# Softmax attention in four stages: dividing the products with the values, one pair of heads at a time, in place of the probabilities

## The chip, the cores and the metric

The kernel runs on one core of a Trainium2 chip. The metric is device time in microseconds (us) for one execution of the whole program.

The engines have short names below: PE is the matrix engine (TensorE), PEld its weight loads, DVE VectorE, ACT ScalarE, POOL GpSimd and SP the engine that issues the loads.

## What is computed

Two small transformer networks run one after the other over 256 context tokens and 256 latent tokens of width 1024. The first has feed-forward layers round two mixers: an even one (global attention beside an RWKV-7 recurrence) and an odd one (window attention with a sink). The second has two mixers: latent attention beside an mLSTM, and gated linear attention (GLA) beside neighbourhood attention. All is in float32, and a product of float32 matrices in the large projections is made of three products of high and low parts.

Each of the four attentions is a softmax over the keys and a product with the values:

```python
def attend(q, k, v):
    s = jnp.einsum('bqhgd,bkhd->bhgqk', q, k).astype(jnp.float32)
    p = jax.nn.softmax(s, axis=-1).astype(v.dtype)
    return jnp.einsum('bhgqk,bkhd->bqhgd', p, v)
```

Three of them scale the products by 1/8, the latent attention by 1/sqrt(96). The window attention has one more logit for each head, the sink, which counts in the sum but has no value.

## The kernel before

One helper, `attend`, makes all four attentions. It is a generator. Its unit of work is one head of a pair and one block of 128 queries, against n keys (256, 384 or 512), so that a pair of heads has four units. For a unit, `scores` makes the products of queries and keys on PE (`ps_s`, L725), takes the maximum of every row on DVE (L730), multiplies it by -scale on DVE (L732, or L734 with a sink), has ACT form the exponentials with their sum (L735), and lets DVE take the reciprocal of the sum (L739) and multiply the unit's 128 x n exponentials by it (L740). Two units later, `turn` transposes these on PE in pieces of 128 x 128 (`ps_ptr`, L751), and ACT copies the result from PSUM (L754). When the four units of a pair are turned, `values` multiplies them with the values on PE (`ps_o`, L760; 128 rows for the pair, 256 queries) and calls the stage's `out`, which takes the result from PSUM: a copy on DVE in the first two stages (L790, L1178), a product with the gate `z` on DVE in the last two (L1452, L1664).

The work is written as generators that take turns (`weave`), and a list scheduler then sets the order of the instructions on each engine. What keeps an order are the data, and the rings of tiles: a pool's tag with `bufs` buffers hands out the next buffer only when its last reader has ended. The tag `nt` of the pool `normp` has four buffers of 128 x 256. In the kernel before it serves the norms (L448), a rotary embedding (`qsw`, L1116), the mLSTM's `u` and `sq` (L1512), and the gates of the last mixer (`zt`, L1627).

The four stages, by the times of the profile:

- Stage 1, 557 to 667 us: 32 units, 16 of 512 keys and then 16 of 256, in turns with `features` of RWKV-7 (L834 to L874, mostly DVE).
- Stage 2, 1779 to 1866 us: 32 units of 384 keys with a sink, in turns with the projection of the queries and half of the output projection (`ps_pr`).
- Stage 3, 2268 to 2382 us: 32 units, 16 of 256 keys and then 16 of 512, in turns with four heads of the mLSTM (`ps_gl` L1474, `ps_sm` L1493, `ps_h` L1506, `ps_ht` L1529) and then the output projection.
- Stage 4, 2594 to 2652 us: 16 units of 512 keys, in turns with the GLA and then the output projection.

These are 112 units and 28 pairs of heads in all.

Of the kernel before, what the change touches and what calls it, by code (L numbers as in the profile page):

```python
# [17 lines left out]
KD = 8  # L18
# [8 lines left out]
def weave(*gens):  # L27
    """run generators in turns; each a generator or (generator, steps per turn)"""
    gens = [g if isinstance(g, tuple) else (g, 1) for g in gens]
    while gens:  # L30
        for g in list(gens):
            for _ in range(g[1]):
                try:
                    next(g[0])
                except StopIteration:
                    gens.remove(g)
                    break


def weave_first(gen, *gens):  # L40
    """all in turns until the first has ended"""
# [6 lines left out]
def every(gen, n):  # L48
    """n steps of gen for one"""
# [5 lines left out]
def until(gen, mark):  # L55
    """the steps of gen as far as the mark; gen can go on from there"""
# [6 lines left out]
class Banks:  # L63
    """pools as one: their tiles in turns"""
# [10 lines left out]
class Net:  # L75
    def __init__(self, es, tc, ins, out):
# [7 lines left out]
        self.hp = p("h", 1)  # the normed stream while a phase multiplies it, other things of its size after  # L84
# [6 lines left out]
    def setup(self):  # L91
# [18 lines left out]
        self.unit = self.const.tile([128, 2, 32], F32, name="unit")  # ones in the first column, in the second  # L110
# [21 lines left out]
    def ring(self, es, raw, split):  # L132
        """for the length of a phase, more of the tiles [128, 1024] that weights go through"""
# [4 lines left out]
    def wtile(self, tag, dt):  # L138
        """in turns from the rings that there are, by their lengths"""
# [11 lines left out]
    def wload(self, w, r0, kt, c0, n):  # L151
        """rows r0.. (kt tiles of 128), columns c0..c0+n of w as (high, low) [128, kt, n]"""
# [12 lines left out]
    def order(self, later, earlier):  # L165
        """the instruction goes after the other one, of the same engine"""
        self.tc.add_manual_dep(later.ins, earlier.ins.name, mybir.DependencyInfo(mybir.DependencyClass.NoSync, mybir.DependencyReason.DATA), reason="order")

    def mm3(self, ps, a, b, first, last):
        """ps += a.T @ b; a, b: (high, low) pairs"""  # L170
# [13 lines left out]
    def proj_steps(self, h, w, c0, ncols, n, done, r0=0, kt=KD, tok=slice(0, 512)):  # L184
        """done(m, psum [128, n]) for each 128 columns of h.T @ w[:, c0:c0+ncols], features on partitions"""
# [14 lines left out]
    def fetch(self, items):  # L200
        """for heads(): items (w, c0, m, done) of 128 columns each"""
        return [(self.wload(w, 0, KD, c0, 128), self.psa.tile([128, 512], F32, tag="a", name="ps_pr"), m, done) for w, c0, m, done in items]

    def heads(self, h, tiles, segs, end=True):
        """done(m, psum [128, 512]) for fetch()'s tiles, the tokens of one segment before those of the next;
        not at the end if other segments follow"""
# [13 lines left out]
    def behind(self, gen, n=99):  # L220
        """n steps of products, on TensorE after what is there so far"""
# [4 lines left out]
    def proj_t_steps(self, h, w, c0, ncols, toks, done, kt=KD):  # L226
        """done(tile, psum [128, ncols]) for each 128 tokens, tokens on partitions"""
# [18 lines left out]
    def opening(self, mod, items, segs):  # L246
        """heads() for the first layer: its modulation vectors in four parts of two tiles of features each, the products of
        a part as it comes"""
# [6 lines left out]
        for f in range(4):  # L255
            ps = self.psm.tile([128, 512], F32, tag="m", name="ps_mod")
            for r in range(2):
                for a in range(2):  # rows of the result: shift or scale, tile, conditioning
# [30 lines left out]
    def mod_steps(self, name, w, fixes, gain=None, start=0):  # L289
        """silu(c) @ w + b for both conditionings to M[name], in steps; fixes: {chunk: (mul, add)}"""  # L290
# [3 lines left out]
        for g in range(start, (nch_all + 3) // 4):  # L294
# [3 lines left out]
            # products and sums over tiles of rows on VectorE; rows: (conditioning, column of a pair), pair  # L298
            for h in range(nch // 2):
                acc = [self.accp.tile([128, 1024], F32, tag=f"acc{i}", name="acc", bufs=1) for i in range(2)]  # L300
                for k in range(KD):
                    v = tile(k, 2 * h)
                    for i in range(2):
                        if k:
                            nc.vector.scalar_tensor_tensor(acc[i], v, cs[:, k, i:i + 1], acc[i], ALU.mult, ALU.add)  # L305
                        else:
                            a = nc.vector.tensor_scalar(acc[i], v, cs[:, k, i:i + 1], None, ALU.mult)
                            if start and (g, h) == (start, 0):  # after opening()
# [32 lines left out]
    def psum(self, es, a, n=1, m=1, x=0, side="left"):  # L341
        """the PSUM pools of a phase: banks for products, norms, modulation, other things"""
# [7 lines left out]
    def tick(self, n=1, left=99):  # L350
        """n steps of the modulation vectors; no group of columns is begun with less than 8 of them left"""
# [13 lines left out]
    def rstd(self, src, ngroups, ones, ntok, eps, dst, psp=None, scale=1.0):  # L365
        """dst [128 tokens, ntok/128, ngroups] = 1 / sqrt(scale * ones' sums of src [128, ntok] (or of several) over partitions + eps)"""
# [11 lines left out]
    def bcast(self, ps, src):  # L378
        """ps [128, 128 tokens] = src [128 tokens, 1] on every partition"""
# [1767 lines left out]
```

## Time and profile before

| | |
|---|---|
| three timed runs | 2671.02, 2678.37, 2682.64 us; median 2678.37 |
| span of the profiled execution, by which all times below are read | 2679.4 us, 1.0 above the median; no other time of it is on record |
| busy over the span: PE, DVE, ACT, POOL | 95%, 66%, 38%, 25% |
| chain of work that ended last: PE, DVE, ACT | 83%, 10%, 3% |

The span is that of one execution under the profiler. The busy share of an engine is a mean over stages that differ, so each of the four stages is read by itself. The granted clock of PE (PEclk) is 1.00 at 2.4 GHz; at its lower level, 1.2 GHz, it is 0.50, and a figure between them is a mean over a stretch in which it had both.

### The profile page before, as it was taken

Reading aid. Unit: us, or ns where it says so; the run is one execution under the profiler, and the core shown is the slowest. Engines: PE = TensorE matmul, PEld = TensorE weight load, DVE = VectorE, ACT = ScalarE, POOL = GpSimd, SP = SyncE. Lnnn points to the kernel's source line nnn. Section 1 sums busy time; section 2 is a strip of 40 time slices with the busy share of each in tenths; the row PEclk is TensorE's granted clock in tenths of the full one; section 3 lists DMA queues with packets and bytes.
Section 4 is the critical chain, followed back from the end, with each engine's and each line's share of the span. In section 5 each row is a group of like instructions: output and inputs, shape, how many; then the busy total and the mean of one; then the engine's idle time right before and its main releaser. Section 6 shows DMA issues by size and latency. Waiting matters only on the chain.

```text
span 2679.4 us, 47406 instructions
## 1 busy us (share of the span) xinstructions
PE 2539.3 (95%) x19372; PEld 2079.3 (78%) x19372; DVE 1764.7 (66%) x2852; ACT 1016.9 (38%) x1916; POOL 672.7 (25%) x665
## 2 busy tenths in 40 slices
PE   7999999998878999999999999999999999999898
PEld 5777789854666887777897777885999887569675
DVE  4967745467666676778586877377554652765885
ACT  3322225345223252222242122366534643645454
POOL 2420322033333143113243113230414120012331
PEclk9999999988787989999999999999999999899999
DMA  8756643100000265566555666241665231023312
GB/s 263 222 175 210 183 123 98 32 0 1 3 4 27 81 180 182 180 194 198 151 149 166 211 186 185 79 132 43 182 186 150 76 103 47 16 67 105 88 48 71
DMA packets 426505, 321.32 MB, mean 120 GB/s; under 512 B 16784, under 2 KB 400528, under 8 KB 426288
## 3 DMA queue, kind: packets, MB, share of 16 engines
q1 hardware_dynamic: 426288, 318.30, 40.5%
q8 instruction: 152, 2.49, 0.4%
q14 instruction: 65, 0.53, 0.1%
HBM read 317.21 MB, written 1.05 MB: 119 GB/s over the span
## 4 chain that ended last, share of the span: by engine, by line
PE 83%; DVE 10%; ACT 3%; issue 2%; DMA 1%; POOL 1%; DVEq 0%; ACTq 0%; SPq 0%; POOLq 0%
PE ps_ff L172 9%; PE ps_ff L173 9%; PE ps_ff L174 9%; PE ps_pr L172 7%; PE ps_pr L173 6%; PE ps_pr L174 6%; PE ps_fo L172 5%; PE ps_fo L173 5%; PE ps_fo L174 5%; PE ps_s L725 3%; PE ps_o L760 2%; PE ps_w L976 2%; PE ps_ptr L751 1%; PE ps_st L1028 1%; DVE wl L157 1%
## 5 line engine op out<-in xcount | busy, mean ns | idle before, releaser
L156 ACT CAST wh<-wr 128x1024 fp32r<-128x1024 f32 (+2 forms) x402 | 417.0, 1043 | 990.5 <-PE ps_ff L173 415.6
L157 DVE TENSOR_TENSOR wl<-wr,wh 128x1024 fp32r<-128x1024 f32 (+2 forms) x402 | 521.4, 1301 | 396.1 <-ACT wh L156 393.0
L172 PE MATMUL ps_ff<-h,wh 128*128 128x512 f32 (+1 forms) x1232 | 451.9, 367 | 0.5 <-ACT fu L536 0.5
L173 PE MATMUL ps_ff<-h,wh 128*128 128x512 f32 (+1 forms) x1232 | 451.1, 366 | 0.0
L174 PE MATMUL ps_ff<-h,wl 128*128 128x512 f32 (+1 forms) x1232 | 450.5, 366 | 0.6 <-DVE wl L157 0.6
L420 POOL TENSOR_SCALAR uh<-fu 128x512 fp32r<-128x512 f32 (+1 forms) x88 | 169.3, 1924 | 774.0 <-DVE fu L537 774.0
L174 PE MATMUL ps_pr<-h,wl 128*128 128x256 f32 (+2 forms) x920 | 305.8, 334 | 12.9 <-DVE wl L157 12.8
L172 PE MATMUL ps_pr<-h,wh 128*128 128x256 f32 (+2 forms) x920 | 305.7, 337 | 7.2 <-ACT wh L156 4.5
L173 PE MATMUL ps_pr<-h,wh 128*128 128x256 f32 (+2 forms) x920 | 305.6, 334 | 2.5 <-POOL h L457 1.5
L305 DVE SCALAR_TENSOR_TENSOR acc<-wr,csa,acc 128x1024 f32<-128x1024 f32 x224 | 296.8, 1365 | 3.9 <-DMA wr<-in_w_mod_dram 3.9
L172 PE MATMUL ps_fo<-uh,wh 128*128 128x512 f32 (+1 forms) x824 | 278.9, 340 | 0.0
L173 PE MATMUL ps_fo<-uh,wh 128*128 128x512 f32 (+1 forms) x824 | 278.7, 339 | 0.0
L174 PE MATMUL ps_fo<-uh,wl 128*128 128x512 f32 (+1 forms) x824 | 277.7, 338 | 0.0
L172 PEld LDWEIGHTS ps_ff<-h,wh 128*128 128x128 f32 x1232 | 231.6, 188 | 51.6 <-ACT wh L156 6.7
L174 PEld LDWEIGHTS ps_ff<-h,wl 128*128 128x128 f32 x1232 | 231.6, 188 | 42.2 <-DVE wl L157 1.0
L173 PEld LDWEIGHTS ps_ff<-h,wh 128*128 128x128 f32 x1232 | 231.7, 188 | 40.5
L174 PEld LDWEIGHTS ps_pr<-h,wl 128*128 128x128 f32 x920 | 177.4, 193 | 30.6 <-DVE wl L157 14.5
L172 PEld LDWEIGHTS ps_pr<-h,wh 128*128 128x128 f32 x920 | 176.9, 194 | 28.0 <-ACT wh L156 8.2
L173 PEld LDWEIGHTS ps_pr<-h,wh 128*128 128x128 f32 x920 | 177.5, 194 | 20.3 <-POOL h L457 2.2
L172 PEld LDWEIGHTS ps_fo<-uh,wh 128*128 128x128 f32 x824 | 155.0, 188 | 26.7 <-issue 8.4
L173 PEld LDWEIGHTS ps_fo<-uh,wh 128*128 128x128 f32 x824 | 155.0, 188 | 18.8 <-issue 0.8
L174 PEld LDWEIGHTS ps_fo<-uh,wl 128*128 128x128 f32 x824 | 154.9, 188 | 18.2
(615 smaller groups left out, 4335.4 us busy)
## 6 DMA issues: line engine op xcount, KB each, us to landing
wr<-in_ffn_in_dram SPq DMA_DIRECT2D x176, 512.0 KB, 4.6
wr<-in_w_mod_dram SPq DMA_DIRECT2D x144, 512.0 KB, 4.4
wr<-in_ffn_out_dram SPq DMA_DIRECT2D x88, 512.0 KB, 4.3
wr<-in_l_w_in_dram SPq DMA_DIRECT2D x55, 512.0 KB, 3.8
wr<-in_l_w_mod_dram SPq DMA_DIRECT2D x48, 512.0 KB, 4.3
wr<-in_even_w_in_dram SPq DMA_DIRECT2D x21, 512.0 KB, 4.1
wr<-in_l_w_out_dram SPq DMA_DIRECT2D x16, 512.0 KB, 4.1
wr<-in_even_w_out_dram SPq DMA_DIRECT2D x14, 512.0 KB, 4.1
```

The costliest lines, as they stand in the source:

```text
L156: a = nc.scalar.copy(hi[:, : kt * n], raw)
L157: b = nc.vector.tensor_tensor(lo[:, : kt * n], raw, hi[:, : kt * n].bitcast(F32), ALU.subtract)
L172: mm(ps, a[0], b[0], start=first, stop=False)
L173: mm(ps, a[0], b[1], start=False, stop=False)
L174: self.mm = mm(ps, a[1], b[0], start=False, stop=last)
L305: nc.vector.scalar_tensor_tensor(acc[i], v, cs[:, k, i:i + 1], acc[i], ALU.mult, ALU.add)
L420: nc.gpsimd.tensor_scalar(hi, src, 1.0, None, ALU.mult)
L725: nc.tensor.matmul(s, q(h, q0s[b]), k(h), start=True, stop=True)
L751: nc.tensor.transpose(tr[:, j * 128:(j + 1) * 128], e[:, j * 128:(j + 1) * 128], self.ident)
L760: nc.tensor.matmul(o[64 * par:64 * par + 64, :nq], v(2 * m + par, j), PT[m, par][:, j, :nq], start=j == 0, stop=j == nk - 1, tile_position ...
L976: nc.tensor.matmul(out(rw, b), lhsT[rw, cl], rhs(rw, cl), start=True, stop=True, tile_position=(32 * q, 32 * q))
L1028: nc.tensor.matmul(Sv[half[par], d, m], TM[h, ks[d], d, m], S[h, par, d, m], start=True, stop=True, tile_position=(64 * (1 - par), 64 * par))
```

## The change

The exponentials stay as they are. The sums of a pair's four units are kept together in a tile `den`, and `values` takes the reciprocals of all four columns at once (DVE, L767 of the changed kernel), spreads each over 64 columns in a tile `rw` (ACT, L769), transposes that on PE into the unused half of the bank of `ps_o` (L771), copies it back to SBUF as `rbs` (ACT, L774), and hands it to `out`. In stages 1 and 2 `out` now multiplies where it copied. In stages 3 and 4 POOL first multiplies the gate by `rbs`, and DVE's product stays. `rw` and `rbs` are tiles of the `nt` ring. In stage 1 the scale 1/8 goes into the gain of the queries, and the maximum is taken with its sign turned, so that the product with -scale falls away there.

Over the program this takes 112 reciprocals and 112 multiplications of exponentials from DVE, and 32 products with -scale. It adds on DVE 28 reciprocals of 128x4, on ACT 56 copies of 128x256, on PE 56 transposes and on POOL 12 products of 128x256. The order of ACT has 34 loads of an activation table where it had 32. Docstrings and comments are gone too, which changes no instruction.

```diff
+            qg8 = T("qg8", [128, 1])
+            nc.vector.tensor_scalar(qg8, qg, 0.125, None, ALU.mult)
...
-                done_q = done_qk(qt, qg)
+                done_q = done_qk(qt, qg8)
...
+        den = {}
...
-            nc.vector.tensor_reduce(mx[:, 0:1], s, AX.X, ALU.max)
-            if sink is None:
+            if (par, b) == (0, 0):
+                den[m] = p.tile([128, len(q0s), 2], F32, tag="den", name="den", bufs=3)
+            total = den[m][:, b, par:par + 1]
+            if sink is None and scale == 1:
+                nc.vector.tensor_reduce(mx[:, 1:2], s, AX.X, ALU.max, negate=True)
+            else:
+                nc.vector.tensor_reduce(mx[:, 0:1], s, AX.X, ALU.max)
+            if sink is None and scale != 1:
                 nc.vector.tensor_scalar(mx[:, 1:2], mx[:, 0:1], -scale, None, ALU.mult)
-            else:
+            elif sink is not None:
                 nc.vector.tensor_scalar(mx[:, 1:2], mx[:, 0:1], -scale, sink[0][:, b, h:h + 1], ALU.mult, ALU.min)
-            nc.scalar.activation(e, s, AF.Exp, scale=scale, bias=mx[:, 1:2], accum_out=mx[:, 2:3])
+            nc.scalar.activation(e, s, AF.Exp, scale=scale, bias=mx[:, 1:2], accum_out=total if sink is None else mx[:, 2:3])
             if sink is not None:
                 nc.scalar.activation(mx[:, 4:6], sink[1][:, b, h], AF.Exp, bias=mx[:, 1:2], accum_out=mx[:, 0:1])
-                nc.vector.tensor_tensor(mx[:, 2:3], mx[:, 2:3], mx[:, 0:1], ALU.add)
-            nc.vector.reciprocal(mx[:, 3:4], mx[:, 2:3])
-            nc.vector.tensor_scalar(e, e, mx[:, 3:4], None, ALU.mult)
...
+            r = den.pop(m)
+            nc.vector.reciprocal(r, r)
+            rw = self.normp.tile([128, 256], F32, tag="nt", name="rw", bufs=4)[:, :nq].rearrange("p (b x e) -> p b x e", x=2, e=64)
+            nc.scalar.copy(rw, r.unsqueeze(3).to_broadcast([128, len(q0s), 2, 64]))
+            for t in range(len(q0s)):
+                nc.tensor.transpose(o[:, nq + t * 128:nq + t * 128 + 128], rw[:, t].rearrange("p g e -> p (g e)"), self.ident)
+            rb = self.normp.tile([128, 256], F32, tag="nt", name="rbs", bufs=4)[:, :nq]
+            turned = o[:, nq:2 * nq].rearrange("p (b q) -> p b q", q=128)
+            nc.scalar.copy(rb.rearrange("p (b q) -> p b q", q=128), turned[:, :, ::-1] if reverse else turned)
             for j in range(nk):
                 for par in range(2):
                     nc.tensor.matmul(o[64 * par:64 * par + 64, :nq], v(2 * m + par, j), PT[m, par][:, j, :nq],
                                      start=j == 0, stop=j == nk - 1, tile_position=(0, 64 * par))
-            out(m, o[:, :nq])
+            out(m, o[:, :nq], rb)
...
-                lambda h, j: va[:, j + (4 - nk), h // 4 * 64:h // 4 * 64 + 64], 0.125,
-                lambda m, o: nc.vector.tensor_copy(qt[m][:, st * 256:st * 256 + 256], o), ring=False)
+                lambda h, j: va[:, j + (4 - nk), h // 4 * 64:h // 4 * 64 + 64], 1,
+                lambda m, o, r: nc.vector.tensor_tensor(qt[m][:, st * 256:st * 256 + 256], o, r, ALU.mult), ring=False)
...
-                                             lambda m, o: nc.vector.tensor_copy(qt[m], o), pre, (nsink, sink), ring=False)
+                                             lambda m, o, r: nc.vector.tensor_tensor(qt[m], o, r, ALU.mult), pre, (nsink, sink), ring=False)
...
+            def out(m, o, r):
                 zs = z[m][:, st * 256:st * 256 + 256]
+                nc.gpsimd.tensor_tensor(zs, zs, r, ALU.mult)
                 nc.vector.tensor_tensor(zs, o, zs, ALU.mult)
...
+        def out(m, o, r):
+            nc.gpsimd.tensor_tensor(z[4 + m], z[4 + m], r, ALU.mult)
             nc.vector.scalar_tensor_tensor(z[4 + m], o, 0.5, z[4 + m], ALU.mult, ALU.mult)
```

The scheduler sets the orders anew in the four stages. The order on DVE in stage 1 is shown first, in the middle of `features` (`cs` to `kt` are its rows, `mx`, `pe` and `ps_s` those of attention). Before:

```order
L732 TENSOR_SCALAR mx<-mx 128x1
L867 TENSOR_TENSOR wr<-t_4353,Ei 128x16x32
L730 TENSOR_REDUCE mx<-ps_s 128x1
L870 TENSOR_TENSOR wr<-t_4354,Ei 128x16x32
L739 RECIPROCAL mx<-mx 128x1
L732 TENSOR_SCALAR mx<-mx 128x1
L740 TENSOR_SCALAR pe<-pe,mx 128x512
L847 SCALAR_TENSOR_TENSOR cs<-reset,sg 128x512
L861 TENSOR_TENSOR ARw<-kk,E 128x16x31
L863 TENSOR_TENSOR ARw<-rt,E 128x16x32
```

After, at the same step of `features` (here L880 is L863 of before, L864 is L847, L738 is L730):

```order
L884 TENSOR_TENSOR wr<-t_4347,Ei 128x16x32
L767 RECIPROCAL den<-den 128x4
L887 TENSOR_TENSOR wr<-t_4348,Ei 128x16x32
L851 SCALAR_TENSOR_TENSOR rk<-rt,c_em_par,kt 128x512
L738 TENSOR_REDUCE mx<-ps_s 128x1 x2
L864 SCALAR_TENSOR_TENSOR cs<-reset,sg 128x512
L711 COPY rb<-kkr 128x512
L891 TENSOR_TENSOR kt<-ps_b,vt 128x512
L738 TENSOR_REDUCE mx<-ps_s 128x1
L878 TENSOR_TENSOR ARw<-kk,E 128x16x31
L880 TENSOR_TENSOR ARw<-rt,E 128x16x32
```

The names with a number are the scratch tiles of `features`. The rows of L732, L739 and L740 are gone from between those of `features`, and one reciprocal of 128x4 has come.

The order on PE in stage 3, at the fourth head of the mLSTM (`ps_sm` and `ps_h`), where attention has reached its heads 5 and 6. Before:

```order
L751 MATMUL ps_ptr<-c_small,wr 128x128 x4
L725 MATMUL ps_s<-k_19435,q_19427 128x512
L1506 MATMUL ps_h<-mv,W 128x129
L725 MATMUL ps_s<-k_19436,q_19428 128x512
L1493 MATMUL ps_sm<-mqk_19442,mqk_20317 128x256 x2
L1506 MATMUL ps_h<-mv,W 128x129 x3
L751 MATMUL ps_ptr<-c_small,wr 128x128 x4
L725 MATMUL ps_s<-k_19436,q_19428 128x512
L751 MATMUL ps_ptr<-c_small,wr 128x128 x4
L760 MATMUL ps_o<-wh,va 64x256
L725 MATMUL ps_s<-k_19437,q_19429 128x512
```

After, at the same head (L1511 is L1493 of before, L1524 is L1506, L1547 is L1529):

```order
L1511 MATMUL ps_sm<-mqk_19412,mqk_20287 128x512
L1524 MATMUL ps_h<-mv,W 128x129 x2
L1511 MATMUL ps_sm<-mqk_19412,mqk_20287 128x512
L1524 MATMUL ps_h<-mv,W 128x129
L1511 MATMUL ps_sm<-mqk_19412,mqk_20287 128x256 x2
L1524 MATMUL ps_h<-mv,W 128x129 x17
L771 MATMUL ps_o<-c_small,rw 128x128 x2
L1547 MATMUL ps_ht<-c_small,mo 128x128 x2
L777 MATMUL ps_o<-wh,va 64x256
L777 MATMUL ps_o<-wl,va 64x256
L777 MATMUL ps_o<-wh,va 64x256
```

Before, the scores, transposes and values of attention stood between the rows of this head (`k_19435` and `k_19436` are the keys of heads 5 and 6). Now the head stands alone from its first `ps_sm` to its last `ps_h`, and the transpose of `rw` comes behind it. After these rows come 48 of the output projection in three pieces, with the values of one more pair and the transposes of one unit between them, and then the rest of attention with no other work between: seven scores, seven units' transposes and the values of three pairs.

## Rows read from the trace of the kernel before

**Rows 1.** The page: span, busy time of each engine, and the chain's shares.

```profile
span 2679.4 us, 47406 instructions
PE 2539.3 (95%) x19372; PEld 2079.3 (78%) x19372; DVE 1764.7 (66%) x2852; ACT 1016.9 (38%) x1916; POOL 672.7 (25%) x665
...
PE 83%; DVE 10%; ACT 3%; issue 2%; DMA 1%; POOL 1%; DVEq 0%; ACTq 0%; SPq 0%; POOLq 0%
```

**Rows 2.** Busy by stretch: PE, PEld, DVE, ACT, POOL; then PEclk, DMA share, GB/s.

```profile
557.00:597.00 40.00, 35.96 (x94) 15.75 (x92) 32.31 (x60) 23.40 (x43) 19.93 (x26) 0.70 0.00 0
597.00:637.00 40.00, 32.05 (x117) 14.74 (x118) 39.30 (x76) 27.52 (x56) 22.70 (x26) 0.92 0.00 1
637.00:667.00 30.00, 28.05 (x156) 14.08 (x155) 17.11 (x66) 14.22 (x49) 0.00 (x0) 0.88 0.00 1
1779.00:1866.00 87.00, 83.66 (x451) 51.52 (x450) 67.35 (x229) 59.39 (x193) 6.22 (x8) 1.00 0.17 50
2268.00:2382.00 114.00, 101.64 (x499) 63.44 (x498) 85.55 (x281) 74.14 (x238) 7.78 (x16) 0.94 0.08 25
2594.00:2652.00 58.00, 52.61 (x365) 30.66 (x364) 39.86 (x108) 30.83 (x66) 1.53 (x4) 0.91 0.14 44
```

**Rows 3.** Groups by line and shape, DVE, 557 to 667 us: busy us, mean ns.

```profile
L740 DVE TENSOR_SCALAR pe<-pe,mx 128x512 f32<-128x512 f32 x16 | 9.3, 599 | 0.1
L740 DVE TENSOR_SCALAR pe<-pe,mx 128x256 f32<-128x256 f32 x16 | 5.6, 351 | 0.3
```

**Rows 4.** The same view of DVE, 597 to 637 us.

```profile
L740 DVE TENSOR_SCALAR pe<-pe,mx 128x512 f32<-128x512 f32 x10 | 6.3, 650 | 0.0
L739 DVE RECIPROCAL mx<-mx 128x1 f32<-128x1 f32 x11 | 1.5, 148 | 0.6 <-ACT pe L735 0.6
L732 DVE TENSOR_SCALAR mx<-mx 128x1 f32<-128x1 f32 x11 | 1.3, 139 | 0.0
```

**Rows 5.** Timeline of PE in stage 2: start us, us, what.

```profile
1821.75 0.55 PE L751 MATMUL ps_ptr<-c_small,pe 128*128 128x128 f32 x3
1822.23 0.91 PE L725 MATMUL ps_s<-ka,q 64*128 64x384 f32 x2
...
1825.94 0.87 PE L751 MATMUL ps_ptr<-c_small,pe 128*128 128x128 f32 x6
1826.75 1.80 PE L725 MATMUL ps_s<-kb,q 64*128 64x384 f32 x4
```

**Rows 6.** Groups by line and shape, 1779 to 1866 us.

```profile
L1119 POOL TENSOR_TENSOR q<-q,c_rope 128x256 f32<-128x256 f32 x4 | 3.1, 774 | 5.2 <-PE ps_sw L1115 5.2
L1178 DVE COPY q<-ps_o 128x256 f32<-128x256 f32 x8 | 3.4, 420 | 6.3 <-PE ps_o L760 6.3
```

**Rows 7.** Groups by line and shape, 557 to 667 us, ACT.

```profile
L754 ACT COPY pt<-ps_ptr 128x256 f32<-128x256 f32 x16 | 5.9, 371 | 9.2 <-PE ps_ptr L751 9.0
L735 ACT ACT_TABLE_LOAD x1 | 1.3, 1283 | 3.5 <-DVE mx L732 3.5
```

**Rows 8.** PE's waits, 2268 to 2382 us: us in total, times, longest us.

```profile
PE ps_s L725 <- ACT wr L735: 4.8, 3, 3.5
PE ps_ht L1529 <- DVE mo L1528: 1.9, 1, 1.9
```

**Rows 9.** Groups by line, 2335 to 2372 us, the mLSTM's fourth head and its neighbours.

```profile
L1506 PE MATMUL ps_h<-mv,W 128*128 128x129 f32 x40 | 5.4, 277 | 0.0
L1498 DVE SCALAR_TENSOR_TENSOR W<-ps_sm,W 128x256 f32<-128x256 f32 (+3 forms) x9 | 3.5, 445 | 0.0
L1493 PE MATMUL ps_sm<-mqk,mqk 128*128 128x512 f32 (+1 forms) x8 | 3.1, 485 | 0.0
```

**Rows 10.** Timeline of PE in stage 4; the bracket is idle time before and its releaser.

```profile
2600.79 0.66 PE L751 MATMUL ps_ptr<-c_small,wr 128*128 128x128 f32 x4
...
2606.42 1.96 PE L725 MATMUL ps_s<-nk,nq 64*128 64x512 f32 x2 [0.81 <-ACT wr L735]
2608.31 1.11 PE L751 MATMUL ps_ptr<-c_small,wr 128*128 128x128 f32 x4
```

More of the change, by code (lines that the diff above doesn't have):

```diff
@@ L729, in scores @@
             mx = p.tile([128, 6], F32, tag="mx", name="mx", bufs=ahead + 2)
-            nc.vector.tensor_reduce(mx[:, 0:1], s, AX.X, ALU.max)
-            if sink is None:
+            if (par, b) == (0, 0):
[6 more added lines that the diff above has]
+            if sink is None and scale != 1:
                 nc.vector.tensor_scalar(mx[:, 1:2], mx[:, 0:1], -scale, None, ALU.mult)
-            else:
+            elif sink is not None:
                 nc.vector.tensor_scalar(mx[:, 1:2], mx[:, 0:1], -scale, sink[0][:, b, h:h + 1], ALU.mult, ALU.min)
-            nc.scalar.activation(e, s, AF.Exp, scale=scale, bias=mx[:, 1:2], accum_out=mx[:, 2:3])
+            nc.scalar.activation(e, s, AF.Exp, scale=scale, bias=mx[:, 1:2], accum_out=total if sink is None else mx[:, 2:3])
             if sink is not None:
                 nc.scalar.activation(mx[:, 4:6], sink[1][:, b, h], AF.Exp, bias=mx[:, 1:2], accum_out=mx[:, 0:1])
-                nc.vector.tensor_tensor(mx[:, 2:3], mx[:, 2:3], mx[:, 0:1], ALU.add)
-            nc.vector.reciprocal(mx[:, 3:4], mx[:, 2:3])
-            nc.vector.tensor_scalar(e, e, mx[:, 3:4], None, ALU.mult)
+                nc.vector.tensor_tensor(total, mx[:, 2:3], mx[:, 0:1], ALU.add)
             E[u] = e
@@ L1449, in mla @@
         for st, n0, nk in ((1, 256, 2), (0, 0, 4)):
-            def out(m, o):
+            def out(m, o, r):
                 zs = z[m][:, st * 256:st * 256 + 256]
+                nc.gpsimd.tensor_tensor(zs, zs, r, ALU.mult)
                 nc.vector.tensor_tensor(zs, o, zs, ALU.mult)
@@ L1661, in pre @@
             nc.vector.scalar_tensor_tensor(sv, nb[:, h, 2 - 2 * b:6 - 2 * b], 8.0, sv, ALU.mult, ALU.add)
-        def out(m, o):
+        def out(m, o, r):
+            nc.gpsimd.tensor_tensor(z[4 + m], z[4 + m], r, ALU.mult)
             nc.vector.scalar_tensor_tensor(z[4 + m], o, 0.5, z[4 + m], ALU.mult, ALU.mult)
```

## The prediction

> **What bounds the kernel now.** The page comes first [rows 1]: PE is busy for 95% of the span and makes 83% of the chain that ended last; DVE is busy for 66%. Read alone, that says that DVE work is hidden and PE work is not. But the change touches four stages of 369 us in all, so the next view is the busy time stretch by stretch [rows 2]. The reader is to look for the engine with the smallest remainder in each row.
>
> - Stage 1 has three parts. From 557 to 597 PE has 35.96 of 40 us at a granted clock of 0.70, DVE 32.31. From 597 to 637 DVE has 39.30 of 40 and PE only 32.05: here DVE is the bound. From 637 to 667 PE has 28.05 of 30, DVE 17.11.
> - Stage 2: PE 83.66 of 87 at a clock of 1.00, DVE 67.35. PE is the bound.
> - Stage 3: PE 101.64 of 114, DVE 85.55, ACT 74.14. PE leads, with 12.4 us idle that are waits for single results [rows 8].
> - Stage 4: PE 52.61 of 58, DVE 39.86.
>
> So DVE's relief should show in the middle of stage 1 and, as shorter chains, a little in stages 3 and 4; in stage 2 it has nothing to shorten.
>
> **What is removed.** In 597 to 637 DVE does ten scalings of 128x512, 6.3 us, eleven reciprocals, 1.5, and eleven products with -scale, 1.3 [rows 4]: 9.1 us. DVE instructions overlap at their edges: 39.30 us of busy time fit in 40 with 76 instructions, so a removed small one frees less than its duration. I take off 0.08 us for each of the 32, an estimate from the busy times (about half of a reciprocal's 0.148): 9.1 - 2.6 = 6.5 us. What DVE gets back here is three or four reciprocals, 0.15 each [rows 4]: 0.6. Net 6.0 us. In 557 to 597 the other six scalings of 512 keys stand, at the mean of 599 ns [rows 3], with as many reciprocals and products with -scale at the durations of [rows 4]: 5.3 us, 3.9 less the overlap of 18. There PE has 4 us idle and the half clock shares the bound, so I count half, 2.0. In 637 to 667 the sixteen scalings of 256 keys, 351 ns each [rows 3], stand beside a PE that has 1.95 us idle; I count 1.0 of that. Together -9.0. The scheduler uses the freed DVE to put more units beside `features`, which moves PE work out of the tail and into PE's idle 8 us of 597 to 637; that is the same gain seen from PE, and not a second one.
>
> In stage 2 thirty-two scalings and reciprocals go, beside a PE that idles 3.3 us in 87: 0. The work that hides them is the products `ps_pr`. With that cover gone (a unit alone), the scaling would be in the unit's chain and its removal would gain.
>
> **What is added.** PE: two transposes for each of the 28 pairs. Three transposes take 0.48 us to the start of the next product and six take 0.81 [rows 5], so one more costs 0.11 and a change of kind about 0.15: two standing alone cost 0.37 us. The changed order shows them alone in most places. Eight pairs: 3.0 us; four: 1.5. The lower bound is two more in a run, 0.22 a pair; the upper is two of 0.185 (0.55 / 3) with a switch on both sides, 0.67.
>
> In stage 1 about three of the eight pairs fall into 597 to 637, where PE has 8 us idle and they cost nothing; five fall where PE leads: +1.9. In stage 2 all eight: +3.0. Stage 3: +3.0. Stage 4: +1.5.
>
> At stage 2 the reading of PE as full can be doubted. The timeline shows its groups starting back to back: the scores start 0.48 us after the three transposes, before these have ended [rows 5], and only 3.3 us of 87 are idle [rows 2]. The Trainium skill, Perfetto Trace Analysis, section Identifying the Most-Contended Engine, says that matmul busy time is no good measure of how near TensorE is to its peak, and that the weight loads' busy share is one; here that is 51.52 of 87, 59% [rows 2]. By that rule the transposes of stage 2 would find room and cost 0 where the rows give 3.0, and the sum would be 3 lower. What a start-to-start reading shows is that the room isn't free to be used, so I keep 3.0.
>
> ACT: two copies of 128x256, 371 ns each [rows 7], 0.74 a pair, 6 us in a stage where ACT has 74 of 114 or less: 0. They do lie in a chain: reciprocal, copy, transposes, copy, product. The changed order issues them before the pair's values, so that the values cover them. Where the cover is gone, at a stage's last pair, one costs 0.15 + 0.37 + 0.37 + 0.37, about 1.3 us less what the last values cover; bound 0 to 1.3 a stage. The two more table loads at 1283 ns [rows 7] fall on ACT in stage 3; 0, at most 2.6. POOL: 12 products of 128x256, 774 ns by the nearest row [rows 6], on an engine that has 7.78 us of work in 114: 0, again but for a last pair. DVE's copy of 128x256, 420 ns [rows 6], becomes a product; the nearest DVE product that reads PSUM takes 445 ns [rows 9], so 0.2 us a stage at most. The 0.125 in the gain is one 128x1 instruction before the stage: 0.
>
> **What is moved.** Stage 3 is the place. `rw` and `rbs` come from the four `nt` buffers that `u` and `sq` of the mLSTM also use, and in the program all the mLSTM's stand ahead of those of the later pairs. So the values of those pairs wait until the mLSTM's last `u` is read; behind them wait the transposed exponentials' buffers, and behind those attention's next units. The order shows it: head 3 of the mLSTM has nothing between its rows on PE. Its chain is `ps_sm` 3.1, the nine products on DVE 3.5, `ps_h` 5.4 [rows 9]; with one bank for `ps_sm` the first two alternate, so PE idles up to 3.5 us that attention filled before, and the normalising after each `ps_h` (seven small instructions on three engines, 0.15 to 0.77 each by [rows 4, 6]) adds 1 to 4.5. I take 5.0; bounds 0 (the next units' transposes fill it after all) and 8.0. Against that go some of the 6.7 us that PE waited for exponentials and for `mo` [rows 8], since DVE has 16 x 0.60 + 16 x 0.35 + 32 x 0.15 = 20 us less to do in 114, by stage 1's durations [rows 3, 4]: -4.0, bounds 0 and -6.7. In stage 4 the same relief: -1.5. In stage 2 the `ps_pr` rows are bunched and two pairs of units run without them; there PE stays led by its own work: +1.0, bounds 0 and 3.
>
> **The sum.** Stage 1: -9.0 + 1.9 = -7.1. Stage 2: +3.0 + 1.0 = +4.0. Stage 3: +3.0 + 5.0 - 4.0 = +4.0. Stage 4: +1.5 - 1.5 = 0. Together +0.9. One thing is left out so far: in stage 1 PE's clock is 0.70 and 0.92 [rows 2]. Less idling there should bring back a part of the roughly 12 us lost by it in the first stretch (0.30 of 40); I put it at -3, bounds 0 and -8. Sum -2.1 against the execution of 2679.4, which stands 1.0 above the median of 2678.37: 2677 in the median's terms.
>
> **The rivals.**
> *Stage 1 gives all.* DVE's relief passes whole (6.0 + 3.9 + 1.95), the clock returns most of its loss (-8), and stage 3 loses nothing by its new order. Stage 1 -18.0, stage 2 +3.0, stage 3 -1.0, stage 4 0: -16, 2662. For it speaks the 39.30 of 40 on DVE; against it that PE is within 4 us of full in the stretch beside it, at whatever clock.
> *Nothing passes.* Every removed DVE instruction was hidden, PE pays for its 56 transposes: 28 x 0.37 = +10, 2689. For it speaks 95% on PE; against it the 8 us that PE idles in 597 to 637.
> *The ring in stage 3 (slower).* Attention stands until the mLSTM has ended: 8.0 for head 3; the units that then run alone, some eight, leave PE 0.5 us idle each if their chains are that much late, 4.5 with the last pair; and PE's clock falls, as in stage 4, where after a wait of 0.81 us the same four transposes take 1.11 us that took 0.66 [rows 10]; ten us of work at the lower clock are +5. In place of 5.0 - 4.0 that is 17.5, so +14.5 in all: 2692. It decides the sign from 3 us more than the 1.0 on, and passes 0.5% at about 16.5. For it speaks the order; against it that PE has the greatest work per unit in the tail, which should keep it fed.
>
> **How the numbers follow.** A measurement of this kernel can tell about 0.5%, 13 us: the three runs lie within 12. Chances: the likeliest, 2677, 0.50, with its own range 2666 to 2687 from the bounds above; stage 1 gives all, 0.22; nothing passes, 0.13; the ring, 0.15. Faster by over 0.5% (under 2665) is most of the second case and an edge of the first, 0.24; slower (over 2691.8) somewhat over half of the last and the edges of two, 0.15; the rest, 0.61, is within. The range 2658 to 2694 holds the first three cases but for the lower edge of the second, and the ring's own figure: it leaves out about 2 in 10.
>
> **What would show it.** Right: DVE in 597 to 637 no longer full, `features` done some 8 us sooner, PEclk there above 0.8; stage 2 three or four us longer with PE at 96% still; in stage 3 a gap on PE in head 3 whose releaser is DVE's `W`, and waits of `ps_o` for `rw` or of POOL and ACT for `nt` buffers. Wrong: stage 2 no longer than before (PE had room), stage 1 unchanged (PE or ACT was its bound), or stage 3 over 12 us longer.

## The result

The changed kernel takes 2703.45 us (median of five runs, 2698.45 to 2705.24), the kernel before beside it 2675.93. The ratio is 1.0082, with a 95% interval of 1.0055 to 1.0109: slower, clear of the noise, and above the upper end of the range that was forecast. Measured once more later (run `again`), it was 1.0074, 1.0057 to 1.0092. (The ratios here and below, as recorded, are not quotients of the two medians, which would give 1.0103; the two ways differ by up to 0.2%.)

The page of the changed kernel, its span and busy times, beside [rows 1]:

```profile
span 2702.7 us, 47307 instructions
PE 2554.6 (95%) x19428; PEld 2086.6 (77%) x19428; DVE 1718.3 (64%) x2625; ACT 1035.8 (38%) x1974; POOL 688.2 (25%) x677
```

DVE has 46 us less to do, PE 15 us more, and the span is 23.3 us longer. The stages by windows, columns as in [rows 2]; the windows are moved and stretched as the stages are in this trace:

```profile
558.00:598.00 40.00, 36.86 (x136) 16.67 (x136) 30.93 (x45) 29.33 (x60) 20.72 (x25) 0.91 0.00 1
598.00:638.00 40.00, 34.79 (x141) 15.74 (x138) 33.45 (x51) 29.61 (x69) 25.29 (x27) 0.89 0.00 1
638.00:664.00 26.00, 25.07 (x126) 13.03 (x128) 5.54 (x15) 10.72 (x36) 0.00 (x0) 0.52 0.00 1
1777.00:1872.00 95.00, 88.68 (x466) 54.70 (x465) 56.23 (x170) 62.76 (x208) 7.87 (x8) 0.91 0.17 47
2278.00:2405.00 127.00, 107.18 (x504) 68.41 (x503) 72.16 (x216) 74.14 (x242) 12.92 (x23) 0.91 0.03 9
2615.00:2675.00 60.00, 53.81 (x374) 30.77 (x375) 32.80 (x83) 34.34 (x77) 4.44 (x8) 0.91 0.14 42
```

In stage 1 DVE is no longer full in the middle (33.45 of 40), as the forecast had it. The surprise is the column of PE's clock: 0.52 in the last part of stage 1, where [rows 2] have 0.88, and 0.91 over stage 2, where they have 1.00. In the last part of stage 1 PE is busy for 25.07 of 26 us, at little more than half its clock. In the first part the clock rose, from 0.70 to 0.91, so that stage 1 as a whole has 41 us at the lower level, where the kernel before has 38.

To see where the 23 us arise, the starts of the same PE products (by tile, operand and count) in the two traces are subtracted, and the median is taken over the 15 us behind each stage. The first row of numbers is the changed kernel; the others are the experiments below. "Low" is how long the profile's clock records show the lower level (1.2 GHz) within that stage; for the kernel before it is 38, 0, 14 and 10 us.

| us against before | stage 1 | to stage 2 | stage 2 | to stage 3 | stage 3 | to stage 4 | stage 4 | low in stages 1, 2, 3, 4 |
|---|---|---|---|---|---|---|---|---|
| changed | -6.1 | +2.6 | +8.5 | +3.0 | +13.8 | -1.7 | +1.4 | 41, 17, 24, 10 |
| again | -6.4 | +0.6 | +6.9 | +3.0 | +14.7 | -2.2 | +1.1 | 41, 14, 24, 10 |
| nodiv | +4.3 | -4.1 | -0.8 | +3.1 | -8.5 | -1.3 | -5.4 | 61, 0, 3, 0 |
| late | -15.1 | -1.8 | +1.2 | +3.2 | +12.2 | -0.2 | -4.4 | 17, 0, 20, 0 |
| own3 | -6.0 | -3.5 | +3.8 | +1.5 | -3.3 | -2.2 | +1.0 | 38, 7, 7, 10 |
| own3_late | -4.8 | -2.1 | +1.2 | +3.2 | +4.1 | -1.9 | -4.2 | 38, 0, 17, 0 |
| bank | -14.1 | -2.9 | +1.8 | +3.0 | +16.6 | -1.6 | -2.8 | 14, 3, 20, 0 |
| own3_direct_late | -13.0 | +1.1 | +2.6 | +1.5 | +0.1 | -2.3 | -4.4 | 10, 0, 7, 0 |
| early1 | -5.9 | +1.1 | +1.2 | +3.1 | +0.5 | -2.7 | -3.8 | 37, 0, 10, 0 |
| early2 | -15.2 | +1.2 | +5.4 | +3.1 | -2.0 | -0.5 | -3.9 | 17, 14, 3, 0 |
| s1 | -6.1 | +2.9 | 0.0 | 0.0 | -0.6 | -2.5 | +3.1 | 41, 0, 10, 17 |

Each row is one execution. Most stand within 2.5 us of their kernel's median, but that of own3 is the shortest of 13, 17 us under its median, and that of own3_late 10 us above its own. The products behind a stage do not all shift alike, most of all behind stage 1, so a single figure is good to 2 or 3 us. The changed kernel loses in stages 2 and 3.

PE's waits in stage 2, all of them, are these (us in total, times, longest us):

```profile
PE ps_s L729 <- ACT pe L745: 1.9, 3, 0.9
PE ps_o L777 <- ACT rbs L774: 1.7, 3, 0.6
PE ps_pr L172 <- ACT oh L416: 1.4, 1, 1.4
PE ps_o L771 <- ACT rw L769: 1.0, 1, 1.0
```

The timeline of PE shows three of them, and what follows (rows as in [rows 5], the bracket is idle time before and its releaser):

```profile
1824.88 0.38 PE L771 MATMUL ps_o<-c_small,rw 128*128 128x128 f32 x2
1825.88 1.52 PE L777 MATMUL ps_o<-pt,va 128*64 128x256 f32 x12 [0.62 <-ACT rbs L774]
...
1833.33 0.55 PE L759 MATMUL ps_ptr<-c_small,pe 128*128 128x128 f32 x3
1834.85 0.44 PE L771 MATMUL ps_o<-c_small,rw 128*128 128x128 f32 x2 [0.97 <-ACT rw L769]
1835.81 0.91 PE L729 MATMUL ps_s<-kb,q 64*128 64x384 f32 x2 [0.52 <-ACT pe L745]
1836.65 0.55 PE L759 MATMUL ps_ptr<-c_small,pe 128*128 128x128 f32 x3
1837.12 1.42 PE L729 MATMUL ps_s<-kb,q 64*128 64x384 f32 x2
1838.47 0.90 PE L759 MATMUL ps_ptr<-c_small,pe 128*128 128x128 f32 x3
1839.30 2.83 PE L777 MATMUL ps_o<-pt,va 128*64 128x256 f32 x12
```

The two transposes of `rw` end, and the values (L777) wait 0.62 us until ACT has copied `rbs`. For the next pair the transposes of `rw` wait 0.97 us for ACT's copy `rw`, and the next scores 0.52 us. Then the granted clock is halved: three transposes that took 0.55 us take 0.90, and the twelve products of a pair 2.83 us where they took 1.52. The trace has 17 us at this level in stage 2, 13.7 of them from 1837 us on, which the kernel before does not have. A wait alone does not bring this about: behind that of 0.62 us at 1814 and behind these two of the kernel before the clock stays at 1.00.

```profile
1837.24 0.91 PE L725 MATMUL ps_s<-kb,q 64*128 64x384 f32 x2 [0.66 <-ACT pe L735]
1840.18 0.91 PE L725 MATMUL ps_s<-kb,q 64*128 64x384 f32 x2 [0.59 <-ACT pe L735]
```

Stage 3 at the mLSTM's last head, the same view:

```profile
2357.10 0.71 PE L1524 MATMUL ps_h<-mv,W 128*128 128x129 f32 x4 [0.78 <-DVE W L1516]
2357.65 1.04 PE L1511 MATMUL ps_sm<-mqk,mqk 128*128 128x512 f32 x2
2359.40 0.49 PE L1524 MATMUL ps_h<-mv,W 128*128 128x129 f32 x2 [0.71 <-DVE W L1516]
2360.00 1.13 PE L1511 MATMUL ps_sm<-mqk,mqk 128*128 128x256 f32 x4
2360.97 0.83 PE L1524 MATMUL ps_h<-mv,W 128*128 128x129 f32 x6
2364.18 3.36 PE L1524 MATMUL ps_h<-mv,W 128*128 128x129 f32 x28 [2.38 <-DVE u L1533]
2371.07 0.69 PE L771 MATMUL ps_o<-c_small,rw 128*128 128x128 f32 x2 [3.52 <-ACT rw L769]
2373.82 0.69 PE L1547 MATMUL ps_ht<-c_small,mo 128*128 128x128 f32 x2 [2.07 <-DVE mo L1546]
```

From 2356 to 2374 us PE waits 0.78, 0.71, 2.38, 3.52 and 2.07 us, 9.5 in all: first for the mLSTM's products on DVE, then for `u` of its normalising, then for `rw`, then for `mo`. Ten us at the lower level follow from about 2370 (the products `ps_pr` behind it take 0.63 us each and later 0.40).

### The profile page after: what moved, and what is told of

It is laid out like the page before. It is cut to its first block, busy times and chain, and to the rows that moved or that the text cites. A ratio compares the mean times of both kernels' runs of the same rounds, so it can differ in the third digit from the quotient of the medians.

```text
span 2702.7 us, 47307 instructions
## 1 busy us (share of the span) xinstructions
PE 2554.6 (95%) x19428; PEld 2086.6 (77%) x19428; DVE 1718.3 (64%) x2625; ACT 1035.8 (38%) x1974; POOL 688.2 (25%) x677
```

## The experiments

The theories were three. A: the chain that stands ahead of a pair's values (reciprocal, copy, transposes, copy) makes PE wait, and PE's clock falls behind that. B: the new order of the units does it, whatever is added. C: the four `nt` buffers tie attention to the mLSTM in stage 3. Times are medians; each is compared with the kernel before, measured beside it on the same chip. The last column is the median time at PE's lower level over a kernel's executions: each has a mean granted clock on record, and twice its shortfall from 1.00, times the span, is that time (to some 3 us).

| | median us | before | ratio, 95% interval | lower level, us |
|---|---|---|---|---|
| changed | 2703.45 | 2675.93 | 1.0082 (1.0055 to 1.0109) | 238 |
| again | 2699.51 | 2679.67 | 1.0074 (1.0057 to 1.0092) | 235 |
| nodiv | 2667.59 | 2679.39 | 0.9939 (0.9916 to 0.9961) | 202 |
| late | 2677.18 | 2679.39 | 0.9972 (0.9948 to 0.9995) | 177 |
| own3 | 2689.10 | 2679.39 | 1.0031 (1.0012 to 1.0049) | 242 |
| s1 | 2679.47 | 2679.39 | 0.9990 (0.9970 to 1.0010) | 217 |
| own3_late | 2665.39 | 2680.85 | 0.9946 (0.9927 to 0.9966) | 170 |
| bank | 2681.52 | 2680.85 | 0.9997 (0.9976 to 1.0018) | 177 |
| own3_direct_late | 2668.25 | 2680.85 | 0.9951 (0.9931 to 0.9970) | 160 |
| early1 | 2676.38 | 2679.67 | 0.9989 (0.9974 to 1.0004) | 198 |
| early2 | 2668.09 | 2679.67 | 0.9959 (0.9944 to 0.9974) | 181 |

The kernel before has 209 us at the lower level by the same median, in each of the three sets of executions beside these kernels. Among executions of one and the same kernel (191 in all, each against its kernel's mean) the time rises by 0.32 us for each us more at the lower level, with a correlation of 0.93.

One thing holds for every edit below that moves work: the scheduler set the orders anew with it. So an edit brings an order of its own in the stages that it touches, beside what it names.

**nodiv: the removal alone.**

```diff
-            r = den.pop(m)
-            nc.vector.reciprocal(r, r)
...
-            nc.scalar.copy(rb.rearrange("p (b q) -> p b q", q=128), turned[:, :, ::-1] if reverse else turned)
...
-            out(m, o[:, :nq], rb)
+            out(m, o[:, :nq])
...
```

> This leaves the division out altogether: the output is that of unscaled sums. It is the removal of DVE work alone, with none of the added instructions. Theory A (the added chain of reciprocal, copy, transposes, copy makes PE idle for short whiles ahead of a pair's values, and PE's granted clock falls for stretches behind them): about 10 us under the kernel before, 2666, stage 2 as before with its clock at 1.00 throughout. Theory B (the new order of the units, which shorter chains bring, idles PE and lowers the clock by itself): stays 8 to 20 us over the kernel before, 2684 to 2696, with stage 2's clock down again. Theory C (stage 3's four nt buffers tie attention to the mLSTM): stage 3 at least 10 us shorter than in the changed kernel, as under A.

Measured: 2667.59, 11.8 us under the kernel before. (The `out`s copy and gate here as they did before.) B falls as the cause of the loss: without the added chain the shorter units cost nothing in stages 2 and 3 (-0.8 and -8.5) and the clock there is up. In stage 1 it is not: this trace has 61 us at the lower level there, the most of all, and +4.3. So what made the changed kernel slower is what was added, with the order that came with it, and it is worth 32 to 36 us by the medians.

**late: the transposes behind the values.**

```diff
-            for t in range(len(q0s)):
-                nc.tensor.transpose(o[:, nq + t * 128:nq + t * 128 + 128], rw[:, t].rearrange("p g e -> p (g e)"), self.ident)
...
-            nc.scalar.copy(rb.rearrange("p (b q) -> p b q", q=128), turned[:, :, ::-1] if reverse else turned)
             for j in range(nk):
...
+            for t in range(len(q0s)):
+                nc.tensor.transpose(o[:, nq + t * 128:nq + t * 128 + 128], rw[:, t].rearrange("p g e -> p (g e)"), self.ident)
...
+            nc.scalar.copy(rb.rearrange("p (b q) -> p b q", q=128), turned[:, :, ::-1] if reverse else turned)
             out(m, o[:, :nq], rb)
```

> The changed kernel with the two transposes of the reciprocals and the copy back behind a pair's products with the values, no longer ahead of them; all else as it was. Theory A: the values no longer stand behind the copy of rbs (six waits of 0.75 us on average in the trace of the changed kernel), stage 2 keeps its clock and is 6 to 8 us shorter, the whole 2690 to 2697. Theory B or C: 2700 to 2706, as the changed kernel.

Measured: 2677.18, some 22 to 26 us under the changed kernel: the direction of A, and far more than the 2690 to 2697 that it gave. Stage 2 stands at +1.2 with its clock at 1.00. PE's waits in this kernel's stage 2 are two:

```profile
PE ps_pr L172 <- ACT oh L416: 1.4, 1, 1.4
PE ps_o L772 <- DVE mx L744: 0.3, 1, 0.3
```

The waits for `rbs` and `rw` are gone here. So is the order: in the changed kernel the twelve products of a pair stand in one run behind the transposes (x12 above); here, and likewise in bank, nodiv and the kernel before, two stand ahead and ten later:

```profile
1799.85 0.65 PE L772 MATMUL ps_o<-pt,va 128*64 128x256 f32 x2
1803.06 1.51 PE L772 MATMUL ps_o<-pt,va 128*64 128x256 f32 x10
1804.50 0.44 PE L775 MATMUL ps_o<-c_small,rw 128*128 128x128 f32 x2
```

No run has the one order with the other's waits, so which of the two costs more is not shown. Stage 3 is nearly as long as in the changed kernel (+12.2): C is a cause of its own.

**own3: buffers of their own in stage 3.**

```diff
-            rw = self.normp.tile([128, 256], F32, tag="nt", name="rw", bufs=4)[:, :nq].rearrange("p (b x e) -> p b x e", x=2, e=64)
+            own = scale == 96 ** -0.5
+            rw = (p.tile([128, 256], F32, tag="rw", name="rw", bufs=1) if own else self.normp.tile([128, 256], F32, tag="nt", name="rw", bufs=4))[:, :nq].rearrange("p (b x e) -> p b x e", x=2, e=64)
...
```

(and the same for `rbs`)

> The changed kernel with buffers of their own for rw and rbs in stage 3 alone (one each); in the other stages they stay with the four nt buffers. Theory C: PE takes attention between the rows of the mLSTM's last head again, stage 3 is 8 to 10 us shorter, the whole 2693 to 2696. Theory A: stage 3 loses mostly by its clock and by single waits, 0 to 4 us shorter, 2699 to 2703.

Measured: 2689.10, some 10 to 14 us under the changed kernel, and below the 2693 to 2696 of C. Stage 3 is at -3.3 in place of +13.8, in the short execution named above; the other rows with buffers of their own have -2.0 to +4.1 there, those in which `rw` and `rbs` share the `nt` ring +12.2 to +16.6. C holds, with a somewhat larger effect than it gave. PE's largest waits in stage 3 of this kernel, to set beside the waits of head 3 in the section on the result:

```profile
PE ps_s L729 <- ACT wr L745: 4.1, 4, 2.6
PE ps_ptr L759 <- ACT wh L762: 1.9, 2, 1.5
PE ps_gl L1493 <- ACT W L1501: 1.9, 1, 1.9
PE ps_h L1525 <- DVE mx L742: 1.1, 1, 1.1
PE ps_o L772 <- ACT u L1536: 0.6, 1, 0.6
```

The waits of 3.52 us for `rw` and of 2.38 for `u` are gone; what waits is spread over single results, as in [rows 8].

**s1: the change in stage 1 alone.**

```diff
+            if not (scale == 1):
+                nc.vector.reciprocal(total, total)
+                nc.vector.tensor_scalar(e, e, total, None, ALU.mult)
             E[u] = e
...
```

> The change in stage 1 alone; stages 2 to 4 divide the exponentials as before (their sums lie in the new tile). By the offsets of the two traces stage 1 gave 2.9 us by the end of the RWKV chain and 6.6 by the end of attention, after a tail of 30 us at the lower clock. Theory A and C: 1 to 5 us under the kernel before, 2671 to 2675, with the same tail at a clock of about 0.5. If the tail's clock were chance of one run and not of the order, it would be 2660 to 2668.

Measured: 2679.47, no difference from the kernel before. That is above the 2671 to 2675 that were expected, though the interval, from 8 less to 3 more, does not exclude them. The tail of stage 1 is at the lower clock again, as expected.

**own3_late: both edits.**

> Both edits on the changed kernel: the transposes and the copy back behind the values, and buffers of their own for rw and rbs in stage 3. The traces of the single edits put stage 1 at -15, stage 2 at +1, stage 4 at -4 (transposes behind the values) and stage 3 at -3 instead of +12 (own buffers). If the two causes are separate these add: 2655 to 2663, 15 to 22 us under the kernel before. If own buffers helped stage 3 only because something else was late there, the sum stays at 2668 to 2677.

Measured: 2665.39, 0.54% under the kernel before and 34 to 38 under the changed one. It lies between the two expectations, 2 us above the one for separate causes. As separate causes they fit: 10 to 14 and 22 to 26 add up to it, within what the medians can tell. This is the fastest of the kernels here, level with nodiv. So the division behind the values costs nothing that these runs can tell, although it still has its 56 transposes on PE.

**bank: the transposes ahead of the values, in another bank.**

```diff
+            ob = pst.tile([128, 512], F32, tag="t", name="ps_rb")
             for t in range(len(q0s)):
-                nc.tensor.transpose(o[:, nq + t * 128:nq + t * 128 + 128], rw[:, t].rearrange("p g e -> p (g e)"), self.ident)
+                nc.tensor.transpose(ob[:, t * 128:t * 128 + 128], rw[:, t].rearrange("p g e -> p (g e)"), self.ident)
...
-            turned = o[:, nq:2 * nq].rearrange("p (b q) -> p b q", q=128)
+            turned = ob[:, :nq].rearrange("p (b q) -> p b q", q=128)
```

> The changed kernel with the transposes of the reciprocals still ahead of the values, but into a tile of the bank that ps_ptr uses, so that the values no longer wait for the copy of rbs out of their own bank. If that wait on the shared bank is what the late placement took away: stage 1 and 2 as there, -15 and +1, the whole 2674 to 2684. If it is the place of the transposes in PE's queue (PE waits for ACT's copy rw before it can go on to the values): as the changed kernel, 2695 to 2705, with PE's waits on ACT rw grown, and stage 3 no better in either case.

Measured: 2681.52, as expected, and stages 1 and 2 at -14.1 and +1.8, as with late. So what costs is not that the transposes come ahead of most of the products: it is that the values write the bank out of which ACT still has to copy `rbs`. Whether the chip needs that wait or only the program's own keeping of order asks for it, no run here separates. Stage 3 is no better (+16.6), as expected.

**own3_direct_late: without the copy `rw`.**

```diff
-                nc.tensor.transpose(o[:, nq + t * 128:nq + t * 128 + 128], rw[:, t].rearrange("p g e -> p (g e)"), self.ident)
+                for par in range(2):
+                    nc.tensor.matmul(o[64 * par:64 * par + 64, nq + t * 128:nq + t * 128 + 128], r[:, t, par:par + 1].to_broadcast([128, 64]), self.ident,
+                                     start=True, stop=True, tile_position=(0, 64 * par))
```

> As own3_late, but without the copy rw: PE spreads the reciprocals itself, four products of a column (repeated 64 times) with the identity for a pair in place of two transposes. That takes 28 copies of 0.37 us from ACT and one step from the chain, and gives PE two more instructions a pair, side by side in the array. If the chain behind the values is hidden: the same as own3_late within 4 us. If it still shows at the ends of the stages: 3 to 6 us less.

Measured: 2668.25, level with own3_late. The copy `rw` is hidden there, and nothing speaks for a cost of the rest of the chain behind the values.

**again, early1, early2: which stage pays for the early placement.** The first is the changed kernel, unedited. The other two start from own3_late; `spread` makes the transposes and the copy back, and early2 has `sink is not None` for the condition:

```diff
+            if scale == 1:
+                rb = spread()
             for j in range(nk):
...
-            rb = spread()
+            if not (scale == 1):
+                rb = spread()
```

> The changed kernel once more, as the measure for the two beside it. 2698 to 2706. If its first figures were chance of one chip, under 2695.

> As own3_late (2665), but with the transposes and the copy back ahead of the values in stage 1 alone. The single placement was worth 26 us over all stages by the medians. Stage 1 by the traces: 9 of them. If the wait in stage 1 costs that (idling and the lower clock at the stage's end): 2672 to 2677. If the clock at the end of stage 1 is chance from one execution to the next, which the trace of own3_late suggests (half clock for 38 us there too): 2664 to 2669.

> As own3_late, but with the transposes and the copy back ahead of the values in stage 2 alone, the stage that PE bounds. By the trace of the changed kernel that costs 7 us there, most of it by 17 us at the lower clock; by that of own3, which has the same order in stage 2, 3 us. So 2668 to 2673. If the wait is nothing where PE is full: 2664 to 2667.

Measured: 2699.51, 2676.38 and 2668.09. By the medians, early placement costs 11 us in stage 1 alone and about 3 in stage 2 alone, the latter inside what two medians can differ by; the trace of early2 has +5.4 there with 14 us at the lower level. The end of stage 1, 628 to 664 us, first of early1, then of early2 (transposes behind the values there):

```profile
628.00:664.00 36.00, 31.68 (x144) 15.88 (x145) 12.12 (x26) 14.86 (x49) 3.01 (x3) 0.57 0.00 1
```

```profile
628.00:664.00 36.00, 28.42 (x205) 15.91 (x204) 21.63 (x42) 17.01 (x54) 4.20 (x6) 0.86 0.00 1
```

PE's clock is 0.57 in the one and 0.86 in the other. In early1 the long stretch at the lower level begins at 632.9 us, behind these two waits:

```profile
631.43 0.41 PE L773 MATMUL ps_o<-c_small,rw 128*128 128x128 f32 x2 [2.60 <-DVE q L815]
632.30 1.44 PE L783 MATMUL ps_o<-pt,va 128*64 128x256 f32 x8 [0.46 <-ACT rbs L776]
```

The transposes wait until DVE has taken the last pair's result out of the bank, and the values wait for `rbs`. The same pair of waits stands at that place in changed, again, own3 and s1, and in all five the stretch begins within 0.6 us of the start of these values. If the stages' costs add, the remaining 10 us or so of the difference between own3 and own3_late fall to stages 3 and 4, where no run separates them; the traces show 5 to 6 of them in stage 4.

One row speaks against reading a single trace too closely. The same stretch of own3_late, whose order in stage 1 is that of late and of early2 on PE, DVE, ACT and POOL:

```profile
628.00:664.00 36.00, 32.83 (x147) 15.12 (x146) 11.33 (x25) 12.62 (x42) 0.00 (x0) 0.57 0.00 1
```

Here the clock was low as well, from 628.9 us, behind waits for exponentials:

```profile
625.79 0.70 PE L729 MATMUL ps_s<-ka,q 64*128 64x256 f32 x2 [0.43 <-ACT pe L745]
627.51 0.70 PE L729 MATMUL ps_s<-kb,q 64*128 64x256 f32 x2 [0.66 <-ACT pe L745]
```

Five traces with early transposes into the values' own bank in stage 1 (changed, again, own3, s1, early1) have 37 to 41 us at the lower level there. Of the five with the transposes behind the values or in another bank, four have 10 to 17 (late, bank, own3_direct_late, early2) and this one has 38. The kernel before has 38 too, and nodiv 61, with no such chain at all. The executions, of which there are more, say it better, over the whole program: with early placement in all stages the median at the lower level is 235 to 242 us (changed, again, own3), with late placement or another bank 160 to 177 (late, own3_late, own3_direct_late, bank); own3_late's trace, with 191, is one of its higher ones. So the placement changes how long the clock stays low, and is not alone in deciding it.

## Why the prediction was wrong

- **The chain ahead of the values ("The changed order issues them before the pair's values, so that the values cover them": 0, and 0 to 1.3 a stage where no cover is left).** This is the step that failed. The values could not cover the copy, because the transposes lie in the bank that the values write: the order put the copy ahead of them, and the order of an engine doesn't show a wait for another engine. By own3 against own3_late it is 24 us over all stages, by bank 18 to 22.
- **The clock.** The sum had -3 for a clock that would come back in stage 1. It came back in the first part (0.91) and fell in the last (0.52), 41 us in all at the lower level against 38: no gain. And the sum had no term for a clock that falls in the other stages. That fall is most of what the chain cost. PE's waits for `rbs` add up to 4.5 us in the whole trace of the changed kernel, and stage 2 has at most some 3 us more idling; but own3 has 242 us at the lower level and own3_late 170, and at the 0.32 us for each us that executions of one kernel show, these 72 us are 23 of the 24. For late and bank it is about 19 of 22 to 26 and of 18 to 22. That the waits bring the clock down is the plain reading of the timelines; no run held them apart from the order that came with them, and executions of one kernel differ too (187 to 259 us in own3), so what else decides the clock stays open.
- **The ring in stage 3 (+5.0, bounds 0 to 8.0).** The mechanism was right, the size was not: the idling at the mLSTM's last head is 9.5 us, ten us at the lower clock follow, and own buffers take 10 to 14 us off the whole. With late placement they take 12 off by the medians, 7 by the ratios, and there the intervals overlap. This was the third rival, whose 2692 stands 7 to 11 us under what was measured. The prediction's own sign of being wrong, stage 3 over 12 us longer, came true (+13.8).
- **DVE's relief.** Right in kind: DVE in the middle of stage 1 went from 39.30 to 33.45 of 40. The terms for it (-9.0, -4.0, -1.5, and -3 for the clock) come to 17.5; the removal alone gave 11.8 us by the medians, and its ratio allows 10 to 23. That they are near is in part luck, for the places differ: nodiv's trace gains nothing in stage 1 (+4.3), where the terms had -12, and 8.5 and 5.4 us in stages 3 and 4, where they had 4.0 and 1.5. Stage 1 gains 13 to 15 us in the traces whose clock stayed up.
- **PE's transposes (0.37 us for each pair, 10 in all).** Probably too dear. nodiv, which has none of them, and own3_late are level (0.9939 and 0.9946), though the two intervals together allow about 10. In stage 2 the traces, whose orders differ too, put the difference at 2.0 (-0.8 to +1.2) where the sum had 3.0. The rule from the Trainium skill, Perfetto Trace Analysis, section Identifying the Most-Contended Engine, was read there as giving 0; the traces lie between.
- **Stage 2's bunching (+1.0).** With the clock up the whole stage costs +1.2 to +2.6, against the +4.0 of the sum.
- **Between stages 2 and 3** every kernel that is changed in stage 2 costs 1.5 to 3.2 us in its trace, where 3 to 7 us at the lower level appear. This was not foreseen, and its cause is not known.

Put together, the relief (-12 to -16 by nodiv), the ring (+10 to +14) and the chain (+24) make +18 to +26; measured were 20 to 28. (The sum of the prediction itself, -2.1 with the 1.0 taken off, gives 2676 and not 2677, which changes nothing.)

## What to carry to other kernels

Before a chain is called covered, ask what the covering work itself waits for: in this kernel it could not hide a copy out of a bank that it was about to write. Small work that is spread from one engine to another did best behind the large work, with buffers of its own; the same 56 transposes and copies cost 24 us ahead of the values and nothing measurable behind them. And a ring of buffers that serves two interleaved pieces of work ties the one to the other's end. One trace can mislead: those of own3 and own3_late show 187 and 191 us at the lower level, where their medians are 242 and 170.

## What the runs showed of the hardware

Waits of half a microsecond to one microsecond on a PE that is otherwise full can cost more than their length: in stage 2 three of them between 1825 and 1836 us, 2.1 us together, were followed by 13.7 us at the lower clock, and the stage is about 7 us longer than in late, which has neither these waits nor the lower clock. Two waits of 0.66 and 0.59 us in the kernel before were not followed by it. PE stayed at the lower level while its busy share was full: 25.07 of 26 us at a clock of 0.52 in the last part of stage 1. Of two kernels with the same order of instructions in that stage, one trace had 17 us at the lower level and one 38 (late and own3_late); executions of one kernel differ by up to 83 us in it over the program (the kernel before, 181 to 264), and each us goes with 0.32 us of time.
